# A hybrid encoder trunk on one core: the state space branch changes layout through memory, the next layer's preparation is cut into small steps, and the tokens are loaded ahead of the weights

## The chip, the cores and the metric

One core of a Trainium2 chip. TensorE (PE) multiplies, VectorE (DVE) and ScalarE (ACT) work on tiles of 128 partitions, GpSimd (POOL) fills and copies a little, SyncE (SP) issues most DMA transfers. The metric is the device time of one execution in microseconds, the median of several runs; a trace of one profiled execution stands beside it.

## The reference

Two layers over 512 tokens of width 1024, all in float32. Each layer is a gated mixer of three branches and a feed-forward part. The branch that the change touches is A, a diagonal complex state space layer of 16 groups of 16 channels:

```python
for l in range(DEPTH):
    h = rms_norm(x, norm1_g[l])
    z = h @ w_in[l]
    (u_ssm, dq, dk, dv, iq, ik, iw, rq, rk, rv, rg, gates) = split_cols(z)
    ya = s5_mixer(u_ssm, ...)        # scan of complex states, then GELU and a gated linear unit
    yb = dsa_mixer(...)              # indexer picks 128 keys per query, attention over them
    yc = retention_mixer(...)        # chunked retention, group norm, gate
    g = jax.nn.sigmoid(gates)
    merged = g_a * (ya @ w_proj_a[l]) + g_b * (yb @ w_proj_b[l]) + g_c * (yc @ w_proj_c[l])
    x = x + merged @ w_out[l]
    h2 = rms_norm(x, norm2_g[l])
    x = x + jnp.square(jax.nn.relu(h2 @ w_ff1[l])) @ w_ff2[l]
return rms_norm(x, final_norm_g)
```

## The kernel before

**Matmuls.** Activations are held feature-major (128 features by 512 tokens). Each product in float32 is made of three in a faster format: every operand is split in a high part and a residue. `wload` (L225) brings a block of weights: a DMA issued by SP into `raw`, a copy by ACT into `wh`, a subtraction by DVE into `wl`. Each of the three has three buffers, so SP can issue a load only when the residue three blocks back is done, and ACT can convert only when TensorE has used the block three back. `fm_blocks` (L261) and `tm_group` (L733) run over such blocks, 24 matmuls each.

**Order.** The order on every engine and queue is fixed at build time by a planner. It plays the program through with durations of its own, and at each point takes the ready instruction of highest priority, which is program order unless `tc.high_priority(n)` moves it ahead by n. Weight loads are moved ahead by 3000 (`LOOK`). A manual dependency of the kind `order` (L98) adds no wait on the chip; it keeps the planner from putting one instruction ahead of another on the same engine.

**Start.** L165 to L173 load constants and the tokens, half of the width by SP and half by ACT, in eight blocks `xt` of 256 KB. They are transposed, scaled and split, and the first projection follows.

**State space branch.** `s5_u` (L645) takes the branch's input from PSUM, 2 blocks of 128 channels by 512 tokens, and scales it by DVE. The state matmuls want another layout: the channels of four consecutive tokens (taps) stacked on the partitions, and the chunks of four tokens on the columns. `shuffle` (L639) makes it in 16 copies of 32 partitions by 128 columns per block, 12 by ACT and 4 by POOL, with a stride of four on the tokens. `s5_states` (L654) runs the state matmuls, the scans and the GELU and ends with the inverse shuffle, again 16 copies per block. `s5_glu` (L711) is the gated unit behind it, and runs after the first attention block, two projections and a top-k search.

In layer 0 the state matmuls come behind that layer's own preparation `s5_prep` (L514): rotation angles with their sines and cosines, and expanded input and output matrices. In layer 1 the preparation has been done during layer 0's feed-forward, and the state matmuls follow the keys directly.

**Feed-forward.** The hidden width is cut into eight slices. `ff1` (L1168) makes half a slice by a scheme of seven products of half size (84 matmuls of 256 columns, four PSUM banks of the pool `mx`, all there are); `ff2` (L1208) multiplies a slice into the residual stream `xp`, in two parts of four output blocks each, with one DVE addition per block (L1214). In layer 0, `s5_prep` for layer 1 is a generator of six steps, and L1258 runs one of them after each slice from the second on. Nothing keeps the planner from taking a step's instructions early.

Of the kernel before, what the change touches and what calls it, by code (L numbers as in the profile page):

```python
# [10 lines left out]
F32 = dt.float32  # L11
# [82 lines left out]
def build(tc, x, positions, norm1_g, w_in, lam_re, lam_im, log_step, b_re, b_im, c_re, c_im, ssm_d,  # L94
          glu_w, glu_b, ret_g, w_pa, w_pb, w_pc, w_out, norm2_g, w_ff1, w_ff2, fin_g, consts, out):
    nc = tc.nc
    pending, last = {}, {}
    order = mybir.DependencyInfo(mybir.DependencyClass.NoSync, mybir.DependencyReason.DATA)  # L98

    class Ordered:  # L100
# [5 lines left out]
        def __getattr__(self, name):  # L106
            fn = getattr(self._e, name)

            def call(*a, **k):
                r = fn(*a, **k)  # L110
                o = k["out"] if "out" in k else a[0]
                tag = pending.pop(o.tensor.name, None)
                if tag is not None:
                    if tag in last:
                        tc.add_manual_dep(r.ins, last[tag], order, reason="pages in program order")
                    last[tag] = r.ins.name
                return r

            return call
# [3 lines left out]
    with es:  # L123
# [4 lines left out]
        def f(t):  # L128
            return t.bitcast(F32)
# [36 lines left out]
        with tc.high_priority():  # L166
# [347 lines left out]
        def s5_prep(l, o):  # L514
# [4 lines left out]
            for hb in range(2):  # L519
# [3 lines left out]
                def v3(z):  # L523
                    return z.rearrange("p (i c) -> p i c", c=NCH)
# [3 lines left out]
                ve.tensor_tensor(v3(t), ib, rl[:, isl, None].to_broadcast([P, 4, NCH]), ALU.mult)  # L528
                ve.tensor_tensor(kk, ang, t, ALU.add)
                ve.tensor_scalar(kk, kk, 1.0 / TWO_PI, MAGIC, op0=ALU.mult, op1=ALU.add)  # L530
                ve.tensor_scalar(kk, kk, MAGIC, None, op0=ALU.subtract)
                for c in PI_PARTS:
                    stt(ang, kk, -c, ang, ALU.mult, ALU.add)
                ve.tensor_tensor(ang, ang, t, ALU.add)
# [21 lines left out]
            ve.tensor_tensor(bb[0], u1, u2, ALU.subtract)  # L556
            ve.tensor_tensor(u1v, bt[1], frb, ALU.mult)
# [16 lines left out]
            def expand(ar, ai, wr, wi, ops, re_t, im_t):  # L574

                for hb in range(2):
                    isl = slice(4 * hb, 4 * hb + 4)
                    sh = [P, 4, TAPS, 16]
                    for z, x1, x2, op in ((re_t[hb], ar, ai, ops[0]), (im_t[hb], ai, ar, ops[1])):
# [4 lines left out]
                        ve.tensor_tensor(w2, x2[:, isl, None, :].to_broadcast(sh), wi[:, isl, :, None].to_broadcast(sh), ALU.mult)  # L584
                        for a in range(2):
                            q = slice(64 * a, 64 * a + 64)
                            ov = z.rearrange("p (i j c) -> p i j c", j=TAPS, c=32)[q, :, :, 16 * a:16 * a + 16]
                            ve.tensor_tensor(ov, w1[q], w2[q], op)

            yield  # L590
            o.car, o.cai = [page(name="car") for _ in range(2)], [page(name="cai") for _ in range(2)]
            expand( ctv[0], ctv[1], prv[:, :, 1:], piv[:, :, 1:], (ALU.add, ALU.subtract), o.car, o.cai)
            vr, vi = [spage(name="vr") for _ in range(2)], [spage(name="vi") for _ in range(2)]
            expand( bbv[0], bbv[1], qrv, qiv, (ALU.subtract, ALU.add), vr, vi)
# [3 lines left out]
            for src, dst in ((vr, o.w1r), (vi, o.w1i)):  # L598
                for hb in range(2):
# [5 lines left out]
                    dst.append(z)  # L605
            yield
# [32 lines left out]
        def shuffle(n, o, i):  # L639
            if n % 4:  # L640
                copy(o, i)
            else:
                gp.tensor_copy(o, i)

        def s5_u(ps_b, b, rb, u):  # L645

            z = spage(name="s5u")
            ve.tensor_tensor(z, ps_b, rb, ALU.mult)
            for i in range(4):
                for j in range(TAPS):  # L650
                    shuffle(4 * i + j, u[32 * j:32 * j + 32, i * P:(i + 1) * P],
                            z[32 * i:32 * i + 32].rearrange("p (c j) -> p c j", j=TAPS)[:, :, j])

        def s5_states(l, o, u):  # L654
            gf = []
            for hb in range(2):
# [47 lines left out]
                for i in range(4):  # L704
                    for j in range(TAPS):
                        shuffle(4 * i + j, g[32 * i:32 * i + 32].rearrange("p (c j) -> p c j", j=TAPS)[:, :, j],
                                s[32 * j:32 * j + 32, i * P:(i + 1) * P])
# [3 lines left out]
        def s5_glu(l, gf, res):  # L711
# [8 lines left out]
            for m in range(2):  # L720
# [7 lines left out]
                copy(h, th, 0.25)  # L728
                stt(lo, th, 0.25, f(h), ALU.mult, ALU.subtract)
# [331 lines left out]
        def layer(l, nrm, o5):  # L1061
# [146 lines left out]
            def ff2(e, part):  # L1208
                hs, ls = sq[e]
                w2 = w_ff2[l][e * 512:(e + 1) * 512]  # L1210
                if e < NE - 1 or l + 1 < DEPTH:
                    for m, ps in fm_blocks(w2, 4 * part * P, 4, hs, ls, mm_ps):
                        m += 4 * part
                        ve.tensor_tensor(xp[m], xp[m], ps, ALU.add)  # L1214
# [38 lines left out]
            for e in range(NE):  # L1253
# [4 lines left out]
                if e:  # L1258
                    next(steps, None)
# [39 lines left out]
```

## Time and profile before

| | us |
|---|---|
| median of three runs | 1496.88 (1495.79 to 1500.19) |
| profiled execution, its own time | 1497.72 |
| its span | 1495.9 |
| TensorE matmuls busy | 1450.0 of the span |
| DVE busy | 1219.5 |
| ACT busy | 697.5 |
| POOL busy | 68.8 |

Times are counted from the start of the span. In a line of the windows the five busy times stand in the order matmuls, weight loads (which overlap them), DVE, ACT, POOL, with the number of instructions in brackets. An engine's idle time in front of an instruction is put down to what released it. A tile is known by the name in the program: `wh` and `wl` are the parts of a weight block, `mm` a product in PSUM, `f` the products of `ff1`, `u` and `s5f` the shuffled input and output of the state space branch, `ang`, `kk`, `pz`, `pw`, `s5m` and `w` tiles of the preparation, `xt` the tokens. A busy TensorE is not TensorE at its peak, so a stretch is also compared with one that does the same matmuls.

### The profile page before, as it was taken

To read this page: it belongs to the slowest core of one execution; us is meant where nothing else is said; L and a number is where in the kernel's file an instruction comes from. 1 tells how busy PE (TensorE), PEld (TensorE's weight loads), DVE (VectorE), ACT (ScalarE), POOL (GpSimd) and SP (SyncE) were. 2 spreads that over 40 slices of the span, in tenths; PEclk is the share of its full clock that TensorE was granted. 3 is DMA by queue.
4 is the path that set the end of the run, shared out by engine and by line. 5 is a ranking of instruction groups with operands and counts; after the bars stand their busy time and mean duration, and the time that the engine had idled before them with its cause. 6 is when DMAs were issued, how large, how long until landed. Compare 5 with 4: busy or idle time off the path is not lost.

```text
span 1495.9 us, 22071 instructions
## 1 busy us (share of the span) xinstructions
PE 1450.0 (97%) x8194; PEld 1279.6 (86%) x8194; DVE 1219.5 (82%) x2612; ACT 697.5 (47%) x1162; POOL 68.8 (5%) x131
## 2 busy tenths in 40 slices
PE   7999999999999999999999999999999999999997
PEld 6888898777887999889888889988788889998897
DVE  6887899985899878987775769998579788778877
ACT  5654643353534343344355753444445444344443
POOL 0311100000010000200001100000000000000000
PEclk9999999999999999999999999999999999999999
DMA  6331222223322333233442223223143323333333
GB/s 216 102 88 40 78 71 71 85 71 116 110 64 86 113 106 100 71 113 99 120 134 73 80 64 99 85 71 85 57 155 92 99 92 99 113 99 101 97 127 114
DMA packets 138992, 144.17 MB, mean 96 GB/s; under 512 B 11834, under 2 KB 131460, under 8 KB 138884
## 3 DMA queue, kind: packets, MB, share of 16 engines
q1 hardware_dynamic: 137556, 140.59, 31.1%
q10 hardware_dynamic: 1328, 2.17, 0.4%
q8 instruction: 64, 1.05, 0.3%
q14 instruction: 44, 0.36, 0.1%
HBM read 136.44 MB, written 6.29 MB: 95 GB/s over the span
## 4 chain that ended last, share of the span: by engine, by line
PE 84%; DVE 8%; ACT 3%; DMA 2%; issue 2%; POOL 0%; SPq 0%; POOLq 0%; DVEq 0%; ACTq 0%
PE mm L110 59%; PE f L110 16%; DVE wl L110 2%; ACT u L110 1%; DMA raw<-in_w_in_dram 1%; PE pv L110 1%; PE mx L110 1%; PE sp L110 1%; DMA raw<-in_w_ff_dram 1%; PE ry L110 1%; PE s5y L110 1%; PE pt L110 1%; ACT wh L110 1%; PE tr L110 1%; DVE raw L110 1%
## 5 line engine op out<-in xcount | busy, mean ns | idle before, releaser
L110 ACT ACTIVATE wh<-raw 128x1024 fp32r<-128x1024 f32 (+4 forms) x318 | 310.4, 978 | 513.3 <-PE mm L110 288.6
L110 DVE TENSOR_TENSOR wl<-raw,wh 128x1024 fp32r<-128x1024 f32 (+4 forms) x318 | 355.0, 1117 | 110.9 <-ACT wh L110 109.4
L110 PE MATMUL f<-xc,wh 128*128 128x256 f32 x1344 | 241.7, 280 | 0.2 <-ACT wh L110 0.2
L110 PE MATMUL mm<-sql,wh 128*128 128x512 f32 (+1 forms) x544 | 205.5, 378 | 1.8 <-DVE sql L110 1.8
L110 PE MATMUL mm<-sqh,wh 128*128 128x512 f32 (+1 forms) x544 | 205.3, 379 | 1.4 <-DVE fft L110 1.1
L110 PEld LDWEIGHTS f<-xc,wh 128*128 128x128 f32 x1344 | 204.7, 188 | 0.4 <-ACT wh L110 0.4
L110 PE MATMUL mm<-sqh,wl 128*128 128x512 f32 (+1 forms) x544 | 204.8, 380 | 0.0
L110 PE MATMUL f<-xc,wl 128*128 128x256 f32 x644 | 173.9, 280 | 0.2 <-DVE wl L110 0.2
L110 PE MATMUL mm<-xgh,wh 128*128 128x512 f32 x384 | 152.3, 397 | 0.0
L110 PE MATMUL mm<-xgl,wh 128*128 128x512 f32 x384 | 151.7, 395 | 0.0
L110 PE MATMUL mm<-xgh,wl 128*128 128x512 f32 x384 | 151.0, 394 | 0.0
L110 DVE TENSOR_TENSOR raw<-raw 128x256 f32<-128x256 f32 (+1 forms) x336 | 106.7, 328 | 28.9 <-DMA raw<-in_w_ff_dram 27.0
L110 PEld LDWEIGHTS mm<-sql,wh 128*128 128x128 f32 x544 | 102.1, 188 | 21.4 <-DVE sql L110 2.4
L110 PEld LDWEIGHTS mm<-sqh,wh 128*128 128x128 f32 x544 | 102.0, 188 | 20.3 <-issue 1.5
L110 PEld LDWEIGHTS f<-xc,wl 128*128 128x128 f32 x644 | 118.2, 188 | 1.2 <-DVE wl L110 0.8
L110 PEld LDWEIGHTS mm<-sqh,wl 128*128 128x128 f32 x544 | 102.2, 188 | 19.5
L110 PE MATMUL mm<-wh,xgh 128*128 128x384 f32 (+1 forms) x320 | 103.2, 336 | 3.4 <-ACT wh L110 2.7
L110 PE MATMUL mm<-wl,xgh 128*128 128x384 f32 (+1 forms) x320 | 105.2, 331 | 0.0
L110 PE MATMUL mm<-wh,xgl 128*128 128x384 f32 (+1 forms) x320 | 102.6, 333 | 1.0 <-DVE xgl L110 1.0
L110 DVE TENSOR_TENSOR x<-x,mm 128x512 f32<-128x512 f32 (+1 forms) x136 | 88.2, 648 | 9.3 <-PE mm L110 8.8
L110 PEld LDWEIGHTS mm<-xgh,wl 128*128 128x128 f32 x384 | 72.4, 188 | 15.4
L110 PEld LDWEIGHTS mm<-xgh,wh 128*128 128x128 f32 x384 | 72.4, 189 | 14.8
(385 smaller groups left out, 2670.5 us busy)
## 6 DMA issues: line engine op xcount, KB each, us to landing
raw<-in_w_ff_dram SPq DMA_DIRECT2D x76, 512.0 KB, 3.4
raw<-in_w_ff_dram SPq DMA_DIRECT2D x112, 256.0 KB, 2.8
raw<-in_w_in_dram SPq DMA_DIRECT2D x52, 512.0 KB, 3.7
raw<-in_w_in_dram SPq DMA_DIRECT2D x32, 384.0 KB, 3.3
raw<-in_w_out_dram SPq DMA_DIRECT2D x16, 512.0 KB, 3.4
xd<-x SPq DMA_DIRECT2D x16, 256.0 KB, 2.2
x<-xd SPq DMA_DIRECT2D x16, 256.0 KB, 4.9
raw<-in_w_proj_c_dram SPq DMA_DIRECT2D x8, 384.0 KB, 3.0
```

The source lines that it names most:

```text
L110: r = fn(*a, **k)
```

## The change

The change has three parts.

*Layout.* `shuffle` goes. `exchange` stores a 128 by 512 block to a tile in device memory and reads it back in four loads of 32 partitions, in runs of 128 numbers, all five issued by SP. The strided access moves to operations that were there: the product in `s5_u` writes its columns tap by tap, and the last operations of `s5_glu` read theirs tap by tap. In between the branch stays in the order of taps.

*Steps.* `s5_prep` is cut by further `yield`s into 35 steps, 33 of which hold work, and one is run after the residual addition of every output block from the second slice on (eight per slice). While a step is traced, `hold` names that addition, and every DVE instruction of the step is ordered behind it. Instructions of other engines are not held.

*Tokens.* The token loads are moved ahead by 100000 instead of the default.

```diff
-    pending, last = {}, {}
+    pending, last, hold = {}, {}, [None]
...
                 r = fn(*a, **k)
+                if hold[0] is not None and self._e is nc.vector:
+                    tc.add_manual_dep(r.ins, hold[0], order, reason="held back")
...
-        with tc.high_priority():
+        with tc.high_priority(100000):
             sc.dma_start(out=ct[:, :P], in_=consts[:, :P])
...
                 ve.tensor_tensor(v3(t), ib, rl[:, isl, None].to_broadcast([P, 4, NCH]), ALU.mult)
+                yield
                 ve.tensor_tensor(kk, ang, t, ALU.add)
                 ve.tensor_scalar(kk, kk, 1.0 / TWO_PI, MAGIC, op0=ALU.mult, op1=ALU.add)
                 ve.tensor_scalar(kk, kk, MAGIC, None, op0=ALU.subtract)
-                for c in PI_PARTS:
+                yield
+                for q, c in enumerate(PI_PARTS):
                     stt(ang, kk, -c, ang, ALU.mult, ALU.add)
+                    if q % 2:
+                        yield
...
             ve.tensor_tensor(bb[0], u1, u2, ALU.subtract)
+            yield
...
                         ve.tensor_tensor(w2, x2[:, isl, None, :].to_broadcast(sh), wi[:, isl, :, None].to_broadcast(sh), ALU.mult)
+                        yield
                         for a in range(2):
                             q = slice(64 * a, 64 * a + 64)
                             ov = z.rearrange("p (i j c) -> p i j c", j=TAPS, c=32)[q, :, :, 16 * a:16 * a + 16]
                             ve.tensor_tensor(ov, w1[q], w2[q], op)
+                        yield
...
-            expand( ctv[0], ctv[1], prv[:, :, 1:], piv[:, :, 1:], (ALU.add, ALU.subtract), o.car, o.cai)
+            yield from expand( ctv[0], ctv[1], prv[:, :, 1:], piv[:, :, 1:], (ALU.add, ALU.subtract), o.car, o.cai)
...
                     copy(z, ps)
                     dst.append(z)
+                    yield
...
-        def shuffle(n, o, i):
-            if n % 4:
-                copy(o, i)
-            else:
-                gp.tensor_copy(o, i)
+        bounce = [tc.dram_tile([P, SEQ], F32, name="bn%d" % q) for q in range(4)]
+
+        def exchange(q, o, z):
+
+            sy.dma_start(out=bounce[q], in_=z)
+            for j in range(TAPS):
+                sy.dma_start(out=o[32 * j:32 * j + 32].rearrange("p (i c) -> p i c", c=NCH),
+                             in_=bounce[q].rearrange("(i p) (j c) -> j p i c", p=32, c=NCH)[j])
+
+        def by_tap(z):
+
+            return z.rearrange("p (c j) -> p j c", j=TAPS)
...
             z = spage(name="s5u")
-            ve.tensor_tensor(z, ps_b, rb, ALU.mult)
-            for i in range(4):
-                for j in range(TAPS):
-                    shuffle(4 * i + j, u[32 * j:32 * j + 32, i * P:(i + 1) * P],
-                            z[32 * i:32 * i + 32].rearrange("p (c j) -> p c j", j=TAPS)[:, :, j])
+            ve.tensor_tensor(z.rearrange("p (j c) -> p j c", j=TAPS), by_tap(ps_b), by_tap(rb), ALU.mult)
+            exchange(b, u, z)
...
                 g = spage(name="s5f")
-                for i in range(4):
-                    for j in range(TAPS):
-                        shuffle(4 * i + j, g[32 * i:32 * i + 32].rearrange("p (c j) -> p c j", j=TAPS)[:, :, j],
-                                s[32 * j:32 * j + 32, i * P:(i + 1) * P])
+                exchange(2 + hb, g, s)
...
-                copy(h, th, 0.25)
-                stt(lo, th, 0.25, f(h), ALU.mult, ALU.subtract)
+                tv = th.rearrange("p (j c) -> p c j", j=TAPS)
+                copy(h.rearrange("p (c j) -> p c j", j=TAPS), tv, 0.25)
+                stt(lo.rearrange("p (c j) -> p c j", j=TAPS), tv, 0.25, f(h).rearrange("p (c j) -> p c j", j=TAPS), ALU.mult, ALU.subtract)
...
-                        ve.tensor_tensor(xp[m], xp[m], ps, ALU.add)
+                        r = ve.tensor_tensor(xp[m], xp[m], ps, ALU.add)
+                        if e:
+                            hold[0] = r.ins.name
+                            next(steps, None)
+                            hold[0] = None
...
-                if e:
-                    next(steps, None)
```

## Rows read from the trace of the kernel before

**Rows 1.** Page part 4, first line: the chain that ended last, by engine.
```profile
PE 84%; DVE 8%; ACT 3%; DMA 2%; issue 2%; POOL 0%; SPq 0%; POOLq 0%; DVEq 0%; ACTq 0%
```

**Rows 2.** Windows: stretch, length, busy time by engine, TensorE clock, DMA share, GB/s.
```profile
0.00:12.90 12.90, 3.94 (x17) 3.23 (x17) 2.48 (x6) 5.49 (x11) 1.81 (x11) 1.00 0.84 274
49.50:52.70 3.20, 1.68 (x10) 1.36 (x8) 0.79 (x4) 3.11 (x9) 0.00 (x0) 1.00 1.01 209
135.00:142.00 7.00, 4.33 (x24) 3.62 (x23) 6.22 (x13) 6.09 (x15) 1.75 (x5) 0.96 0.00 0
200.00:300.00 100.00, 97.79 (x494) 83.59 (x494) 98.06 (x254) 39.26 (x77) 4.04 (x4) 1.00 0.28 83
450.00:460.00 10.00, 6.95 (x28) 4.66 (x26) 10.00 (x23) 4.18 (x7) 0.00 (x0) 1.00 0.22 67
800.00:805.00 5.00, 2.72 (x17) 2.40 (x15) 0.58 (x1) 4.87 (x12) 0.00 (x0) 1.00 0.37 105
1210.55:1231.43 20.88, 20.88 (x135) 18.90 (x134) 16.82 (x30) 8.62 (x12) 0.00 (x0) 1.00 0.32 97
```

**Rows 3.** Timeline of the start: start us, us, engine, operation, [idle before <-releaser].
```profile
0.74 1.49 SPq L110 DMA_DIRECT2D raw<-in_w_in_dram  x3
...
6.01 0.47 SPq L110 DMA_DIRECT2D xt<-in_x_dram  x1
...
7.56 3.35 ACTq L110 DMA_DIRECT2D xt<-in_x_dram  x4
...
12.93 0.41 PE L110 MATMUL mm<-wh,xgh 128*128 128x292 f32 x1 [0.77 <-ACT xgh L110]
```

**Rows 4.** Tiles u and s5f: count, ns min/median/max, first and last start.
```profile
L110 ACT ACTIVATE u<-s5u x48: 420/427/444, 40.9 to 803.8; 32x128 f32<-32x128 f32 x48
...
L110 ACT ACTIVATE s5f<-s5g x48: 422/428/441, 135.8 to 855.8; 32x128 f32<-32x128 f32 x48
```

**Rows 5.** Timeline of DVE in layer 0: two waits for ACT.
```profile
52.64 0.29 DVE L110 TENSOR_TENSOR iks<-z,iks 128x128 fp32r<-128x128 f32 x1 [2.42 <-ACT iks L110]
...
172.47 0.55 DVE L110 TENSOR_TENSOR qs<-qT,qs 64x384 fp32r<-64x384 f32 x1 [3.26 <-ACT qs L110]
```

**Rows 6.** Chain in order of time: start us, length us, engine and tile.
```profile
354.45 55.16 PE mm L110 x239
...
700.10 1.75 PE w L110 x16
...
722.74 9.89 PE f L110 x84
...
743.63 3.49 PE kk L110 x32
...
1084.03 71.00 PE mm L110 x308
...
1440.33 9.90 PE f L110 x84
```

**Rows 7.** Groups on DVE, 410 to 760 us: first and last of the preparation.
```profile
L110 DVE SCALAR_TENSOR_TENSOR ang<-kk,ang 128x512 f32<-128x512 f32 x8 | 5.3, 672 | 0.0
...
L110 DVE TENSOR_TENSOR pz<-ct,vec 32x256 f32<-32x256 f32 x1 | 0.4, 422 | 0.0
```

**Rows 8.** Page part 6, DMA issues: count, KB each, median us to landing.
```profile
raw<-in_w_in_dram SPq DMA_DIRECT2D x32, 384.0 KB, 3.3
...
xd<-x SPq DMA_DIRECT2D x16, 256.0 KB, 2.2
...
pz<-in_ssm_b_re_dram SPq DMA_DIRECT2D x2, 64.0 KB, 4.1
```

**Rows 9.** Waits: engine and tile, waited for, us in total, times, longest.
```profile
SPq L110 <- DVE wl L110: 1025.0, 253, 20.2
...
ACT wh L110 <- DMA raw<-in_w_in_dram: 3.0, 3, 2.0
```

**Rows 10.** Timeline of ACT in layer 1: the first input copies.
```profile
792.82 5.30 ACT L110 ACTIVATE u<-s5u 32x128 f32<-32x128 f32 x12 [2.86 <-DVE s5u L110]
```

More of the change, by code (lines that the diff above doesn't have):

```diff
@@ L588, in expand @@
                             ve.tensor_tensor(ov, w1[q], w2[q], op)
+                        yield
             yield
             o.car, o.cai = [page(name="car") for _ in range(2)], [page(name="cai") for _ in range(2)]
-            expand( ctv[0], ctv[1], prv[:, :, 1:], piv[:, :, 1:], (ALU.add, ALU.subtract), o.car, o.cai)
+            yield from expand( ctv[0], ctv[1], prv[:, :, 1:], piv[:, :, 1:], (ALU.add, ALU.subtract), o.car, o.cai)
             vr, vi = [spage(name="vr") for _ in range(2)], [spage(name="vi") for _ in range(2)]
-            expand( bbv[0], bbv[1], qrv, qiv, (ALU.subtract, ALU.add), vr, vi)
+            yield from expand( bbv[0], bbv[1], qrv, qiv, (ALU.subtract, ALU.add), vr, vi)
             yield
```

## The prediction

> **What bounds the kernel now.** I read the page's chain first: TensorE's own work is most of the chain that ended last [rows 1]. So the time is TensorE's matmuls plus the places where it stands still, and only those places can give anything back. I then cut the span into stretches and looked for a PE busy time below the length of the stretch. In the feed-forward part of layer 1, a pitch (one block of 84 matmuls of 256 columns and one of 48 of 512) takes 20.88 us with PE busy for all of it [rows 2]. That is the rate to aim for. Losses stand where the change works: before the first matmul, 12.9 us with 3.94 busy; 3.20 us with 1.68 while ACT moves the state space input of layer 0; 7.00 with 4.33 while it moves the state space output; 5.00 with 2.72 at the same place in layer 1; 10.00 with 6.95 at the start of layer 0's feed-forward, where DVE is busy for all 10.00 [rows 2]. Between 200 and 300 us DVE is busy for 98.06 of 100, with the top-k search and the weight residues: there DVE sets the pace, so in the stretch ahead of it the time that counts is DVE's idle time, not PE's [rows 2].
>
> **Tokens first.** Now SP issues three weight loads, then three token blocks, and the fourth token block only at 6.01; ACT issues the other half at 7.56, behind its weight conversions; the first projection matmul comes at 12.93 [rows 3]. Afterwards all eight token blocks are issued by about 3 us, at 0.4 to 0.5 each on two queues, and the weights follow. The stretch moves 274 GB/s [rows 2]. Ahead of the first weight tile stand 2.10 MB of tokens, 0.07 MB of constants and the tile's own 0.30 MB: 2.47 MB at 274 GB/s is 9.0 us, from about 1.8 us on, so it lands at 10.8; with 0.7 for its conversion (an estimate) the first matmul stands at 11.5: 1.4 us gained. The token side alone (first transposes wait for a block issued 5.3 us late) would give up to 4. I take -2 between -4 and +1 (the tile lands late). The Trainium skill, "DMA: Bandwidth & Descriptors", section "Issuing engines are not separate DMA queues", says that loads issued by SP and ACT run on the same engines and interleave; this is the sum above. Were ACT's half on a path of its own, only 1.4 MB would stand ahead of the tile, and the gain would be near the 4. No row here separates the two.
>
> **State space input, layer 0.** Removed: per layer 24 ACT copies of 427 ns (10.3 us) and 8 on POOL, which is idle [rows 4]. The ACT copies hold back the key copies; DVE waits 2.42 us for them, and PE loses 1.5 us in that stretch [rows 2, 5]. The consumer of the moved data is far away (the first state matmul comes after all of layer 0's preparation), so the path through memory is covered by that work; without this cover it would cost its whole latency, worked out below. I take -2.1, between -2.4 and +2.
>
> **State space output, layer 0.** The same 24 ACT copies, at 428 ns [rows 4]. The first twelve stand in front of a weight conversion (PE loses 2.7 us in that stretch), the second in front of the query copies: DVE waits 3.26 us [rows 2, 5]. DVE sets the pace afterwards, so I count DVE's idle time, 3.3, and of PE's 2.7 at the first place 2.1, since other copies of ACT stand there too: -5.4, between 0 and -8 (a further stall of TensorE behind the late query copies goes as well). The consumer, the gated unit, stands behind two projections and a top-k search in program order: covered.
>
> **What an exchange costs.** One store of 256 KB and four loads of 64 KB, all on SP. The store's row is the one of x to memory: 2.2 us to landing; the loads write runs of 512 bytes, and their bound above is the 64 KB load in runs of 64 bytes, 4.1 us, below the store's 2.2 [rows 8]. I take 3. With issues of 0.4 each [rows 3] the data are there 0.4 + 2.2 + 1.6 + 3 = 7.2 us after the product, and SP is held for 4.2 us, as the loads wait for the store. Queued behind on SP stand the weight loads. They are issued when a raw buffer comes free, three conversions ahead; so two blocks lie between issue and conversion, 24 matmuls each: 2 x 5.5 us at 512 columns (a pitch less its 84 short matmuls, for 48 [rows 2, 6]), 2 x 4.1 at 384, less 3.3 for the landing [rows 8]: 7.7 and 4.9 us of slack. SP spends 1025 us waiting for such buffers, and ACT waited only 3.0 us for projection weights [rows 9]. One exchange is therefore hidden; two in a row, 8.4 us, exceed the smaller slack by 3.5. DVE and ACT now read strided operands in the input products and in the gated unit. No row prices that at 512 columns; between nothing and a doubling of eight DVE operations as wide as the angle steps, 672 ns [rows 7], it is 0 to 5 us on DVE. I take 0, as these stand beside matmuls.
>
> **State space input, layer 1.** Here the consumer is near. The first product ends at 792.82, where the copies start, and the last copy starts at 803.8 [rows 4, 10]. After the change SP does two exchanges in a row, so the second block is there at 792.8 + 4.2 + 7.2 = 804.2: no earlier. But ACT is free for the key and weight copies, and TensorE has the query projection to do. It loses 2.3 us now [rows 2]. I take -1.5, between -2.6 and +4 (matmuls ordered behind the data, or weights late by those 3.5). The output copies of layer 1 stand beside a TensorE that is busy throughout: nothing.
>
> **Preparation in steps.** Both layers run the same code from the last branch projection to the end of the 14th block of 84 matmuls. In layer 1, without preparation, from 1084.03 to 1450.23: 366.2 us. In layer 0 from 354.45 to 732.63: 378.2 [rows 6]. Of the 12.0 us more, 1.75 are sixteen transposes, true work [rows 6], and 0.4 are four more of that size: 9.8 us is what crowding costs. The angle work of both halves runs at the start of the feed-forward, where DVE is full. After the change each DVE operation of a step is ordered behind the residual addition of an output block, from the second of the eight hidden slices on. Queued behind it on DVE are the weight residues, for which TensorE waits. All the preparation is 33.1 us of DVE in 21 rows (first and last shown), 15.4 of it the angles [rows 7]. A pitch has room for 20.88 - 16.82 = 4.1 us [rows 2]. 33 steps with work in them, four to a pitch, ask for 4.0 on average: it fits, just. The ten angle steps ask for 15.4 in 2.5 pitches, 2.1 us too much in each, 5.2 in all; the weight residues lie ahead in priority and in buffers, and the angle work itself is not urgent. I take -7, between -9.8 and 0. The last step (small matmuls, 3.49 us on the chain, after the last block of 84 now [rows 6]) moves in among those blocks, which need all four of its PSUM banks: +1, between 0 and +4. The preparation's four 64 KB loads move with it; they take SP some 0.5 each to issue, as the tokens do, and land in 4.1 [rows 3, 8]: within the slack above. Its fills and copies on POOL meet an idle engine.
>
> **The sum.** -2 - 2.1 - 5.4 - 1.5 - 7 + 1 = -17.0 us against the profiled execution's 1497.72 (span 1495.9), which lies 0.8 us above the median of 1496.88. That is 1480.7; I say 1481. Ends of all terms together: -26.8 and +11.
>
> **The rivals.** First, *SP is held* (slower). A store can stand at the head of SP's queue before its product is ready, because the order on SP is fixed at build time. If it stands there 6 us, each of eight exchanges holds SP for 10.2 us, 3.9 beyond the mean slack of 6.3: +31 us, 1512. It decides from 2.1 us beyond the slack for each, where it eats the 17. For it speaks that SP is a queue of waits already; against it that weights arrive long before use [rows 9]. Second, *DVE has no room* (small gain): angles and residues collide, so the preparation gives half (-3.5), the last step costs 2, and half of the copies' 9.0 returns as waits for DVE between 200 and 300 us: -2 - 4.5 - 3.5 + 2 is -8: 1490. For it speaks the 4.0 against 4.1; against it that the angle work is now done where DVE has no room at all. Third, *all stalls go*: every term at its good end but the start's, -24.8: 1473. Fourth, *the change does not do what it says*, the angle work staying where it is: then the preparation gives nothing, -11.0 with nothing paid for the last step, 1487, beside the second and counted with it.
>
> **How the numbers follow.** Forecast 0.58; SP held 0.12; DVE has no room 0.18; all stalls go 0.12. Around each lies the reordering of every queue, which I cannot price, some 5 us. The range 1466 to 1497 leaves out most of the first rival and little below. A difference under 0.3%, 4.5 us, can't be told from no change. Faster: 0.58 + 0.12 + two thirds of 0.18, 0.82. Same: the rest of the second and a little of SP's, 0.08. Slower: 0.10.
>
> **What would show it.** Right: the first projection matmul near 11.5; no PE loss near 50 and 140; from the last branch projection of layer 0 to its 14th block under 372 us; angle work spread behind output blocks; weights never late after an exchange. Wrong: ACT or TensorE waiting for weight loads behind a store, state matmuls waiting for their input, a DVE full through the feed-forward with TensorE waiting for residues, or a hole at the last step.

## The result, and the profile after

The changed kernel takes 1487.64 us (median of 4 runs, 1487.29 to 1488.78) against 1496.34 us for the kernel before beside it: a ratio of 0.9926, with an interval of 0.991 to 0.9942. The profiled execution of after took 1487.64 us with a span of 1485.9, 10.0 us below the span of before. The forecast was 1481 us, 16 us less than before: the direction holds and the time lies in the range, but only half to two thirds of the gain came (8.7 us between the two medians, 11 by the ratio).

First the chain that ended last, by engine (page part 4, first line, of after). VectorE's part went from 8% to 4% [rows 1]; TensorE's own work is now nearly all of it.

```profile
PE 91%; DVE 4%; ACT 2%; DMA 2%; issue 1%; POOLq 0%; ACTq 0%; SPq 0%; DVEq 0%
```

Then stretches of after: length, then busy time and instructions of PE, PEld, DVE, ACT and POOL, the granted TensorE clock, DMA share, GB/s.

```profile
40.00:60.00 20.00, 20.00 (x118) 19.55 (x117) 20.00 (x80) 10.85 (x23) 2.69 (x2) 1.00 0.61 160
126.00:136.00 10.00, 9.69 (x63) 8.99 (x62) 3.22 (x6) 3.17 (x6) 0.00 (x0) 1.00 0.07 27
200.00:300.00 100.00, 100.00 (x497) 85.08 (x497) 97.60 (x241) 42.86 (x83) 4.92 (x3) 1.00 0.30 86
432.43:442.43 10.00, 10.00 (x86) 9.99 (x85) 9.59 (x15) 5.89 (x8) 0.00 (x0) 1.00 0.34 105
560.40:582.04 21.64, 21.15 (x135) 18.96 (x134) 19.54 (x39) 8.51 (x13) 0.53 (x1) 1.00 0.33 98
673.32:680.00 6.68, 6.68 (x46) 6.68 (x46) 2.35 (x8) 3.22 (x12) 0.00 (x0) 0.75 0.24 78
800.00:805.00 5.00, 5.00 (x31) 5.00 (x30) 4.61 (x7) 1.06 (x1) 1.04 (x2) 1.00 0.16 32
1242.48:1263.36 20.88, 20.88 (x133) 18.90 (x132) 17.11 (x31) 8.51 (x12) 0.00 (x0) 1.00 0.35 108
```

The holes named in [rows 2] are gone: nothing is lost between 40 and 60, nothing at 800, and the feed-forward of layer 0 begins with a full TensorE (432.43 to 442.43). New are three things. At 126 VectorE does 3.22 us of work in 10. A pitch in the middle of layer 0's feed-forward takes 21.64 us, where layer 1 still takes 20.88. And behind the last step the granted clock is 0.75 over 6.68 us.

The same in milestones. This is the chain of after in order of time (start, length, what), to be laid beside [rows 6]; the last two lines are from TensorE's timeline, the first matmul of the last branch projection in either layer.

```profile
669.96 3.54 PE kk L110 x32
...
716.86 9.89 PE f L110 x84
...
1430.64 9.90 PE f L110 x84
```
```profile
347.88 0.50 PE L110 MATMUL mm<-ybh,wh 128*128 128x512 f32 x1 [1.22 <-ACT ybh L110]
...
1074.14 0.50 PE L110 MATMUL mm<-ybh,wh 128*128 128x512 f32 x1 [1.22 <-ACT ybh L110]
```

Up to the last branch projection of layer 0 the kernel gained 6.6 us (354.45 to 347.88 [rows 6]); from there to the one of layer 1 it gained 3.3 (729.6 to 726.3); behind it nothing. This middle length, **from branch projection to branch projection**, holds all of the preparation, wherever its steps lie, and the mixer of layer 1; it is the measure for most experiments below.

### The profile page after: what moved, and what is told of

It is laid out like the page before. It is cut to its first block, busy times and chain, and to the rows that moved or that the text cites. A ratio compares the mean times of both kernels' runs of the same rounds, so it can differ in the third digit from the quotient of the medians.

```text
span 1485.9 us, 22022 instructions
## 1 busy us (share of the span) xinstructions
PE 1453.9 (98%) x8194; PEld 1282.3 (86%) x8194; DVE 1220.4 (82%) x2612; ACT 660.8 (44%) x1068; POOL 51.6 (3%) x99
## 4 chain that ended last, share of the span: by engine, by line
PE 91%; DVE 4%; ACT 2%; DMA 2%; issue 1%; POOLq 0%; ACTq 0%; SPq 0%; DVEq 0%
PE mm L110 64%; PE f L110 17%; PE mx L110 1%; PE pv L110 1%; PE sp L110 1%; DVE wl L110 1%; PE ry L110 1%; PE tr L110 1%; DMA xt<-in_x_dram 1%; PE pt L110 1%; PE s5y L110 1%; ACT wh L110 1%; PE rs L110 0%; PE kk L110 0%; DVE s5t L110 0%
## 5 line engine op out<-in xcount | busy, mean ns | idle before, releaser
L110 PEld LDWEIGHTS mm<-xgl,wh 128*128 128x128 f32 x384 | 72.4, 188 | 14.7
```

## Experiments

Each kernel stands beside runs of the kernel before on the same chip, and ratios are to those. A ratio of 0.001 is 1.5 us. Single profiles need care: a second profile of after, unchanged, reached its branch projection 3.8 us earlier and took 3.0 us more from there to the next. The first of these differences is TensorE's granted clock, as the stretch up to the branch projection shows in the two profiles, the first profile above:

```profile
0.00:347.88 347.88, 332.00 (x1728) 290.08 (x1728) 296.50 (x806) 164.37 (x317) 30.34 (x55) 0.98 0.33 96
```
```profile
0.00:344.12 344.12, 327.37 (x1728) 285.50 (x1728) 296.37 (x806) 164.33 (x317) 28.82 (x55) 0.99 0.33 97
```

The same 1728 matmuls kept TensorE busy 4.6 us longer at 0.98 than at 0.99; its idle time, length less busy, is 15.9 and 16.8 us. So idle time is compared below beside length. What rests on one stretch is shown in several kernels, or left as a hint.

The clock moves whole executions too. Over the 68 executions of the kernel before that stand beside the experiments, a mean clock lower by 0.001 goes with about 1.0 us more (an estimate, from a straight line through their recorded times and clocks). The mean clock of the executions of before lies between 0.990 and 0.992 on each chip, that of the other kernels between 0.992 and 0.996, so some us of a ratio can go with the clock. Whether a kernel raises its clock itself, or met it by chance, was not tested.

**The three parts alone.** The first kernel is before with one edit:

```diff
-        with tc.high_priority():
+        with tc.high_priority(100000):
```

> The kernel before with one edit alone: the token loads ahead of the weights. Theory 1 (the start gains what the trace of after shows by 30 us, 1.5 us, and nothing later gives it back): 1494.8 us. Rival (the first matmul comes earlier, but VectorE or ScalarE sets the pace of the first 60 us, so the gain is spent before the state space input ends): 1496.3, no change.

Measured: 0.9974 (0.9961 to 0.9987), 3.9 us less: more than Theory 1's 1.5, and the rival is out. The second is before with `exchange`, `by_tap` and the reordering in `s5_glu`, and nothing else of the diff (shortened; `[...]` stands for the indices):

```diff
-                    shuffle(4 * i + j, u[...], z[...])
+            exchange(b, u, z)
...
-                    shuffle(4 * i + j, g[...], s[...])
+                exchange(2 + hb, g, s)
```

> The kernel before with the state space input and output passed through memory, and nothing else. Theory 1 (the copies' stalls of layer 0 go as the trace of after shows: 2.3 us near 50, 2.9 near 140; layer 1 gives at most 1): 1490.5 us. Rival A (SP is held: in after it stands at a store of the state space output 24.3 us in three places, and this takes back what the copies gave): 1494 to 1497. Rival B (the layout is worth the whole change, the steps nothing): 1488.

Measured: 0.9964 (0.9951 to 0.9977), 5.4 us less, close to Theory 1's 5.8; both rivals lie outside. The third is before with the added `yield`s, `hold` and the loop of `ff2`, and nothing else (the `yield`s and `hold` are as in the diff of the change):

```diff
+                        if e:
+                            hold[0] = r.ins.name
+                            next(steps, None)
+                            hold[0] = None
...
-                if e:
-                    next(steps, None)
```

> The kernel before with the preparation of layer 1 in small ordered steps, and nothing else. Theory 1 (the steps remove the pile of angle work at the start of the feed-forward, but each held operation of VectorE stands ahead of a weight sum that ScalarE and TensorE wait for, so of 9.8 us only 2 to 3 come back): 1493.5 us. Rival A (the steps give the forecast 7 less 1, and it is the layout that gave little): 1490. Rival B (VectorE has no room at all, the steps cost as much as they free): 1496 or more.

Measured: 0.9981 (0.9967 to 0.9994), 2.8 us less, Theory 1's number; both rivals are out. The three add up to 12.1 us, within the interval of the whole (8.7 to 13.5). So no disturbance between the parts can be seen, though each part is known only to some 2 us. The tokens gave the forecast 2 us or more (1.9 to 5.8), the layout 5.4 of 9.0 and the steps 2.8 of 6.

**Which half of the layout.** From the layout kernel, the input goes back to copies (indices shortened):

```diff
-            ve.tensor_tensor(z.rearrange("p (j c) -> p j c", j=TAPS), by_tap(ps_b), by_tap(rb), ALU.mult)
-            exchange(b, u, z)
+            ve.tensor_tensor(z, ps_b, rb, ALU.mult)
+            for i in range(4):
+                for j in range(TAPS):
+                    shuffle(4 * i + j, u[...], z[...])
```

> The kernel before with the state space output alone passed through memory; the input is copied as before. Theory 1 (the output gives half of the layout's 5.4: in the trace of after VectorE's wait for the query copies is gone, but a wait for the state matmuls behind projections of TensorE stands in its place): 2 to 3 us less than before, a ratio of 0.998. Rival (the output gives what was forecast, 5.4, and the input nothing): 0.9964, as the whole layout.

Measured: 0.9993 (0.9978 to 1.0009): no difference. The rival's 0.9964 is out; Theory 1's 0.998 lies at the edge of the interval. The other half has the input through memory, and the output copied and `s5_glu` reading as before (indices shortened):

```diff
-                exchange(2 + hb, g, s)
+                for i in range(4):
+                    for j in range(TAPS):
+                        shuffle(4 * i + j, g[...], s[...])
```

> The kernel before with the state space input alone passed through memory; the output is copied as before. Theory 1 (the layout's gain, a ratio of 0.9964, is the input's, since the output alone gave 0.9993; in the first 60 us VectorE has no idle time left to give back later): 0.997, some 4 us less than before. Rival (each half alone only moves a wait, and the two pay together): 0.999 or more.

Measured: 0.992 (0.9897 to 0.9943), some 12 us by the ratio and 5.9 in the span of its profile, whose execution was its longest. The rival falls. Theory 1 has the direction; its size of 4 us is too small by the ratio. But about half of the 12 us goes with the clock: the mean clock of these executions is 0.9957, that of the kernel before beside them 0.9900, worth some 5.7 us by the estimate above. The layout kernel and its kernel before both have 0.9924. At equal clock the input alone gives some 6 us and both halves 5.4, so the gap between 0.992 and 0.9964 is no measure of what the output costs.

What holds is this: **the layout's gain is the input's; the output alone gives nothing that can be measured.** Two views show what the output's way through memory costs. First its price, by tiles (count, ns min/median/max, first and last start). In the kernel with the input alone:

```profile
L110 ACT ACTIVATE yah<-s5q x4: 612/630/679, 194.6 to 926.7; 128x512 fp32r<-128x512 f32 x4
L110 DVE SCALAR_TENSOR_TENSOR yal<-s5q,yah x4: 679/683/683, 196.3 to 927.7; 128x512 fp32r<-128x512 f32 x4
L110 DVE TENSOR_TENSOR s5u<-mx,rbc x4: 1071/1077/1131, 40.9 to 792.3; 128x512 f32<-128x512 f32 x4
```

and in the kernel with the output alone:

```profile
L110 ACT ACTIVATE yah<-s5q x4: 1104/1134/1222, 198.6 to 932.2; 128x512 fp32r<-128x512 f32 x4
L110 DVE SCALAR_TENSOR_TENSOR yal<-s5q,yah x4: 1048/1060/1086, 200.6 to 934.0; 128x512 fp32r<-128x512 f32 x4
...
L110 DVE TENSOR_TENSOR s5u<-mx,rbc x4: 672/684/691, 40.8 to 794.9; 128x512 f32<-128x512 f32 x4
```

The product in `s5_u` now reads operands that step over four elements of 4 bytes, 16 bytes; the two operations in `s5_glu` read, tap by tap, with a step of 128 elements, 512 bytes. Each costs VectorE 0.38 to 0.39 us more and ScalarE 0.50: 3.1 and 2.0 us over both layers. The Trainium skill, "SBUF — State Buffer", section "Door 1: The DMA port swizzle (why `[64,N]` ≈ `[32,N]`)", states that an access pays when it crosses to a new line of 16 bytes; with a step of 16 bytes or more every element does, and these rows agree. The product also reads from PSUM, and no run here separates the two memories.

Second, layer 1. The windows below are 16 us of its attention, from 33 to 17 us ahead of its last branch projection: the input alone, then the output alone.

```profile
1045.69:1061.69 16.00, 15.25 (x79) 12.88 (x78) 10.44 (x21) 9.19 (x19) 0.00 (x0) 1.00 0.17 53
```
```profile
1053.42:1069.42 16.00, 14.70 (x74) 11.85 (x72) 8.99 (x19) 8.42 (x18) 0.00 (x0) 1.00 0.23 70
```

With the output in memory TensorE does five matmuls fewer in this window, with 0.55 us less busy and at the same clock, with VectorE's work around it in another order (19 operations, not 21). The same cut gives 14.5 to 14.7 in the profiles of all eight other kernels with the output in memory, after among them, and 15.25 in before and in the two others that copy it. From the start of the 14th block of 84 matmuls in layer 0 to this branch projection before takes 361.4 us (722.58 to 1084.03), the input alone 358.7 (720.04 to 1078.69), the output alone 363.8 (722.64 to 1086.42), and two kernels with both and the same work in this stretch 363.1 (layout) and 362.0 (late last step, below). So in layer 1 the output costs some 2 us alone and 3.3 to 4.5 on top of the input; in the layout kernel a lower clock is part of it. That the build arrives at another order is shown; why it does was not tested.

**Is SP held?** This is after with the exchanges on POOL's queue:

```diff
-            sy.dma_start(out=bounce[q], in_=z)
+            gp.dma_start(out=bounce[q], in_=z)
```

and so for the four loads.

> The kernel after with the eight exchanges through memory issued from POOL's queue instead of SP's; nothing else. Theory 1 (SP's stands at these stores and loads, 24.3 us for three products and 13.2 us for data to land, cost nothing, as ACT waited only 4.4 us for projection weights): 1487.6 us, within 1.5. Rival (SP is held, the weights queued behind it come late and the output's half of the layout gave only 2 to 3 us instead of 5.4 for that reason): 1484 to 1485.

Measured: 0.9922 (0.9903 to 0.9942), as after. The waits of after say why: SP does stand at the head of a store for up to 9.6 us, as the first rival had it, but the weights behind it come in time.

```profile
SPq L110 <- DVE s5g L110: 24.3, 3, 9.6
...
ACT wh L110 <- DMA raw<-in_w_in_dram: 4.4, 2, 3.1
```

ScalarE waited 4.4 us for projection weights where it waited 3.0 before [rows 9]. The mechanism of that rival exists; its price does not.

**What the steps lack: the tie, the last step, or room?** First, after without the tie:

```diff
-                            hold[0] = r.ins.name
                             next(steps, None)
-                            hold[0] = None
```

> The kernel after without the tie of each step behind its output block's residual addition; the small steps, their place in the program, layout and tokens stay. Theory 1 (the tie puts the preparation's work between the sums of the next weights on VectorE, and a hole of some 2 us in each of five pitches comes from that order): faster than after, 1478 to 1483, and the holes at the blocks of 84 matmuls gone. Rival (the price is the work itself, and without the tie the angle work runs early where VectorE is full): 1490 or more, with TensorE waiting at the start of the feed-forward again.

Measured: 0.9938 (0.9921 to 0.9956); my theory named 1478 to 1483 us, and it is 1490. It falls. The first two pitches take 22.9 and 23.5 us again, as the rival said (20.9 in after): the tie does what it is for. Next, the last step back behind the last block (`count` starts at 0):

```diff
-                            next(steps, None)
+                            if count[0] < 34:
+                                next(steps, None)
+                            count[0] += 1
```

> The kernel after with one edit: the last step of the preparation (the sixteen small matmuls into one bank and what follows them) stays behind the last output block, as in the kernel before; the other 34 steps as in after. Theory 1 (in after the granted clock falls right behind these small matmuls, 0.75 over 6.68 us, and the pitch takes 1.6 us more; behind the last block of 84 matmuls it did not fall in the kernel before): 1486.0 us, 1.6 less than after, and no pitch behind them above 20.9. Rival (the clock falls wherever they stand, or the tail of the layer exposes what follows them): 1487.6 or more.

Measured: 0.9916 (0.9898 to 0.9935), no different from after. The two pitches behind the old place of these matmuls are back at 20.9 us in its profile, as Theory 1 said, but its 1.6 us is less than the interval can show. A second profile of after shows that the clock is not the whole price:

```profile
672.93:679.60 6.67, 5.70 (x48) 5.52 (x48) 2.36 (x8) 3.22 (x12) 0.00 (x0) 1.00 0.24 79
```

and, from the waits of the same stretch:

```profile
PE f L110 <- DVE s5m L110: 1.0, 1, 1.0
```

Here the clock stayed at 1.00 behind the same matmuls, yet TensorE stood still for 0.97 us until VectorE had emptied the last step's PSUM bank, and the pitch took 22.2 us instead of 22.5. In the first profile, at the lower clock, TensorE comes to that bank later and does not wait. So, by these two profiles, the slower clock mostly fills a wait. Both together are 1.3 to 1.6 us, and the kernel without them gains less than can be measured. Now fewer steps to a pitch, first five of each eight output blocks, then six:

```diff
-                        if e:
+                        if e and m in (0, 2, 4, 6, 7):
```

> The kernel after with the 35 steps spread over all 56 output blocks, five to each eight instead of eight, so that two and a half instead of four fall into a pitch; the last step falls behind the last block of 84 matmuls. Theory 1 (VectorE has no room: 16.8 us of its own work and 3.8 of steps fill a pitch of 20.9, and the pitches with steps take 21.7): with 2.4 us of steps the pitches come back to 20.9 to 21.1, 3 to 4 us less, and the clock's 1.6 as well: 1482.5 us. Rival (it is the order, a held operation ahead of a weight sum, and not the amount, so more pitches pay less each): 1486, only the clock's part.

Measured: 0.988 (0.986 to 0.99), 1483.2 us, beside 1487.5 for the kernel with the late last step on the same chip, at nearly the same mean clock (0.9940 and 0.9935). Theory 1 has the number; the rival's 1486 is out. Of thirteen pitches in its profile, its shortest execution, ten take 20.9 us, the others 21.3, 21.6 and 22.6.

```diff
-                        if e:
+                        if e and m in (0, 2, 3, 4, 6, 7):
```

> The kernel after with the steps on six of each eight output blocks instead of all, three to a pitch; the last step falls right behind the last block of 84 matmuls. Theory 1 (VectorE's room in a pitch decides, 4.1 us: four steps ask for 3.8 on average and more where they are angle work, three ask for 2.85): nearly all of what the spreading over five of eight gave, pitches of 20.9 to 21.2, 4 to 6 us less than after. Rival (any held step ahead of a weight sum costs some 0.2 us, however many stand in a pitch): half of it, pitches of 21.4, 2 to 3 us less than after.

Measured: 0.9897 (0.9878 to 0.9917), 1484.5 us, on one chip with after itself:

> The kernel after itself, unchanged, so that the other kernels of this call stand beside it on one chip. Every theory expects a ratio of 0.991 to 0.994 to the kernel before.

Measured: 0.9912 (0.9892 to 0.9933), 1487.0 us. So three to a pitch gives 2.4 us on the same chip. That is the rival's 2 to 3 us and not Theory 1's 4 to 6, and from the sixth on its pitches take 20.9 to 22.3 us, not 20.9 to 21.2. In the order of steps per pitch, four, three, two and a half, the middle length is 726.3 to 729.3 (after, twice) and 726.6 (late last step), 725.2, 721.7. Fewer tied steps in a pitch, less time: this is shown. That it is because VectorE has no room is not. Windows of the spread kernel, two pitches in the same place as 560.40 to 582.04 above:

```profile
533.10:554.01 20.91, 20.91 (x133) 18.93 (x132) 19.43 (x36) 9.77 (x15) 0.00 (x0) 1.00 0.32 101
554.01:575.29 21.28, 21.28 (x138) 19.11 (x136) 20.86 (x42) 9.62 (x15) 0.00 (x0) 1.00 0.31 99
```

VectorE is as busy in the first as in the 21.64 of after (19.43 and 19.54), and TensorE loses nothing. Two more pitches say it more strongly: one of after that holds 6.0 us of angle steps (its rows with `ang`, `angt` and `kk`), more than any other pitch of after, and one of the kernel with three to a pitch, which holds 2.3 us of steps (its rows with `pw`).

```profile
495.10:515.99 20.89, 20.89 (x134) 18.91 (x133) 20.17 (x37) 10.51 (x14) 0.00 (x0) 1.00 0.39 105
```
```profile
599.33:620.91 21.58, 21.19 (x133) 18.98 (x132) 18.96 (x38) 8.65 (x12) 0.00 (x0) 1.00 0.33 101
```

The fuller pitch loses nothing, the emptier one 0.7 us. So neither VectorE's share of a pitch nor the amount of steps against the 4.1 us of room tells a good pitch from a bad one. Where the work stands does; this is the timeline of after in the pitch from 560.40, VectorE, then ScalarE, then TensorE (start, length, operation, idle time before):

```profile
562.38 0.42 DVE L110 TENSOR_TENSOR raw<-raw 128x256 f32<-128x256 f32 x1
...
564.52 1.08 DVE L110 TENSOR_TENSOR wl<-raw,wh 128x896 fp32r<-128x896 f32 x1
565.52 0.84 DVE L110 TENSOR_TENSOR cai<-pw 64x256 f32<-64x256 f32 x2
566.40 0.62 DVE L110 TENSOR_TENSOR raw<-raw 128x128 f32<-128x128 f32 x2
568.08 3.38 DVE L110 TENSOR_TENSOR wl<-raw,wh 128x896 fp32r<-128x896 f32 x3 [1.07 <-ACT wh L110]
...
567.10 3.10 ACT L110 ACTIVATE wh<-raw 128x896 fp32r<-128x896 f32 x3 [5.83 <-issue]
...
568.11 1.06 PE L110 MATMUL f<-xc,wh 128*128 128x256 f32 x7 [0.49 <-ACT wh L110]
```

The three sums of one weight tile (`raw<-raw`) begin at 562.38 and end at 567.02. Between them stand two residues and a residual addition (left out above), a weight residue and a step (`cai`). VectorE has no gap in all that time; ScalarE has been idle for 5.83 us when it converts the tile at 567.10, and TensorE waits 0.49 of the pitch's extra 0.76 us for it. The trace names no releaser for ScalarE ("issue"), but the sums that it reads end 0.08 us earlier. Once the tile is converted, VectorE itself waits 1.07 us. In the bad pitch of three to a pitch the same order stands, with `car` for `cai`:

```profile
604.73 0.84 DVE L110 TENSOR_TENSOR car<-pw 64x256 f32<-64x256 f32 x2
605.60 0.62 DVE L110 TENSOR_TENSOR raw<-raw 128x128 f32<-128x128 f32 x2
...
606.31 1.90 ACT L110 ACTIVATE wh<-raw 128x896 fp32r<-128x896 f32 x2 [4.94 <-issue]
...
607.31 1.21 PE L110 MATMUL f<-xc,wh 128*128 128x256 f32 x8 [0.39 <-ACT wh L110]
```

In both a step of 0.84 us stands just ahead of the last sums of a weight tile, and TensorE waits 0.39 to 0.49 us for that tile. That is the "order" of the rival to the spreading. It is read from two traces; no kernel moved a step within a pitch to test it, so why fewer steps in a pitch cost less stays open: fewer may simply come to stand in such a place.

Last, the spread kernel without the tie:

> The spread kernel (steps on five of each eight output blocks) without the tie of each step behind its block's residual addition. Theory 1 (the tie's use is to keep the angle work out of the first two pitches, where without it TensorE lost 4.6 us in the trace): 2 to 4 us more than with the tie, 6 to 7 less than after at best. Rival (spread out in the program, the steps need no tie): within 1 us of the spread kernel, 7 to 8 us less than after.

Measured: 0.9938 (0.9918 to 0.9958), 1490.2 us, 3.2 more than after and 5.6 more than three to a pitch on the same chip. Its first two pitches take 23.9 and 23.5 us. The rival falls, and Theory 1 was still too mild: without the tie the spreading gains nothing (1490.1 us for four to a pitch without the tie, on another chip). The tie alone does gain: after took 1487.0 us, 3.2 less than this kernel on its chip. **The spreading pays only with the tie.**

The spread kernel is the fastest that ran: its interval (0.986 to 0.99) lies below that of after in the first result (0.991 to 0.9942) and just overlaps that of after beside three to a pitch (0.9892 to 0.9933); the ratios differ by some 5 to 7 us. Spreading with the input alone in memory was not run.

## Why the prediction came out as it did

The time lies in the range, and the terms can be set in two groups. Ahead of the branch projection of layer 0 the forecast took 9.5 us (tokens 2, input 2.1, output 5.4); the two profiles of after gained 6.6 and 10.3 there, and TensorE's idle time fell by 9.3 and 8.4. Behind it the forecast took 7.5 (1.5, 7, less 1); the profiles gained 3.3 and 0.3. So most of what is missing is missing behind the branch projection. The sum ahead of it came out by luck: one term gave more, another less. The forecast has no term for the granted clock, with which some 4 of the 13.2 us of after beside three to a pitch go (mean clock 0.9947 against 0.9906, by the estimate above).

*Tokens first*, -2 taken, 3.9 measured alone (1.9 to 5.8). The step "all eight token blocks are issued by about 3 us" is wrong, as the start of after shows against [rows 3]:

```profile
0.74 1.80 SPq L110 DMA_DIRECT2D xt<-in_x_dram  x4
1.66 1.28 ACT L110 ACT_TABLE_LOAD   x1 [1.66 <-PEq L1302]
2.58 2.65 SPq L110 DMA_DIRECT2D raw<-in_w_in_dram  x3
4.29 0.90 ACTq L110 DMA_DIRECT2D xt<-in_x_dram  x2
...
5.24 2.47 ACTq L110 DMA_DIRECT2D xt<-in_x_dram  x2
...
10.08 1.34 PE L110 MATMUL mm<-wh,xgh 128*128 128x292 f32 x4 [0.72 <-ACT wh L110]
```

ACT issues its tokens behind its own instructions, from 4.29 to 7.7, so the weight tile probably had less in front of it than I put there: the first projection matmul comes at 10.08, not 11.5. With the tokens alone TensorE's idle time ahead of the branch projection of layer 0 falls from 25.1 to 21.0 us. The size was off on the good side, for a reason I did not have.

*State space input, layer 0 and layer 1*, -2.1 and -1.5 taken: right in direction and about in size. These are the stretches up to the branch projection of layer 0 in before, with the input alone, and with the output alone:

```profile
0.00:354.45 354.45, 329.31 (x1728) 288.71 (x1729) 296.40 (x806) 181.09 (x363) 33.48 (x71) 0.98 0.30 88
```
```profile
0.00:351.65 351.65, 329.15 (x1729) 288.54 (x1729) 296.44 (x806) 173.68 (x341) 30.94 (x63) 0.99 0.31 92
```
```profile
0.00:354.17 354.17, 331.26 (x1728) 290.02 (x1728) 297.63 (x806) 171.83 (x339) 28.67 (x63) 0.98 0.31 91
```

With the input alone the branch projection comes 2.8 us earlier, and TensorE's idle time falls by 2.6, from 25.1 to 22.5. The middle length falls by 2.5. The hole at 800 is gone, and ScalarE waited for projection weights for 2.5 us, no more than before.

*State space output, layer 0*, -5.4 taken: this step failed. Alone the output moves the branch projection of layer 0 by 0.3 us. TensorE's idle time falls by 2.2 us, to 22.9, not by 5.4; and its 1728 matmuls are busy 1.95 us longer than in before, at a lower clock: the granted clock reads 0.50 from 183 to 189 us in that profile, and 0.51 over only 3.5 us, from 182.40, in before. VectorE's wait for the query copies did go [rows 5]. But I added VectorE's 3.3 us and TensorE's 2.1 as if what comes behind were free. In the trace of after VectorE waits in the same part for something else. These are its waits from 106 to 179.5 (us in total, times, longest):

```profile
DVE s5g L110 <- ACT s5g L110: 4.6, 2, 3.9
...
DVE gate L110 <- PE mm L110: 3.3, 2, 2.1
```

In before the first was 3.6 and the second 1.3 us. With the output alone, though, they are 3.6 and 1.9: there new waits take back only 0.6 us. So part of the loss is the clock, part is waits that differ from kernel to kernel, and the rest stays open. I had said that VectorE sets the pace from 200 on; ahead of that the two take turns: TensorE was busy for 9.69 of the 10 us from 126 in after, while VectorE had 3.22 us of work. For a stall that goes I asked what is late next, and answered without reading who has work left.

*State space output, layer 1*, nothing taken: it cost some 2 us, by the stretch from the 14th block to the branch projection (363.8 for 361.4). *Strided operands*, bounded by 0 and 5 us and taken at 0: 3.1 us on VectorE. The bounds were right; the choice is doubtful, for half of the operations stand in layer 0, and the first of them where VectorE is full (20.00 of the 20 us from 40). What they cost the kernel was not measured apart.

*What an exchange costs*, 7.2 us from product to data: right in size. The DMA issues of after for the output (KB each, median us to landing) are

```profile
bn<-s5g SPq DMA_DIRECT2D x4, 256.0 KB, 2.0
s5f<-bn SPq DMA_DIRECT2D x16, 64.0 KB, 2.0
```

and with four issues of 0.43 us between them the first block of layer 0 is there some 6 us after its store is issued.

*Preparation in steps*, -7 taken, and +1 for the last step: 2.8 measured alone (0.9 to 4.9). The pile at the start went as forecast; it was 5.7 us in two pitches (23.92 and 23.52 for 20.88), of the 9.8 counted as crowding; before has four later pitches of 22.2 to 22.6 as well, and after has its own. The step that failed is "33 steps with work in them, four to a pitch, ask for 4.0 on average: it fits, just". It weighs an amount against idle time, and that decides nothing in either direction. Of the angle steps, for which I feared 2.1 us too much in each pitch, 6.0 us cost nothing in one pitch (495.10 to 515.99) and 5.4 us cost 0.8 in the next, as much as 3.2 us of other steps did in three later pitches (21.6 to 21.8). What a step stands ahead of in VectorE's queue fits the traces better. The prediction's own sign failed too: from the last branch projection of layer 0 to the end of its 14th block it wanted under 372 us, and after takes 378.9 (347.88 to 726.75), or 375.3 without the small matmuls (3.54) that moved in, against 378.2 before. The last step was sized well: it does meet the banks it was said to meet (1.0 us), but moved away it changed nothing that can be measured.

*The rivals.* "DVE has no room" has the sum: the preparation gave half, and the copies' gain came back in part. Its 1490 is 2.4 us from the measured time, the forecast 6.6. But it put the returned waits between 200 and 300 us, where TensorE is busy for 100.00 of 100 in after, and it feared the angles, of which 6.0 us cost nothing in a full pitch. So its number is partly luck. "SP is held" was right that SP would stand at a store that is not ready, and wrong that anything waits for it. "The change does not do what it says" has the nearest number of all, 1487, and is out: the angle work moved. That is luck.

## What to carry to other kernels

Work that is tied to places in a full queue is not priced by its sum against the idle time: spread it thinly, keep the tie, and look at what each piece stands ahead of and who waits for that. When a stall is taken from one engine, find the engine that is a little later in the same stretch before counting the gain, and try the halves of a symmetric change one by one, since one may pay for the other. Before a few us are put down to an edit, compare the granted clock of the executions. A changed layout that makes a neighbour read or write with a stride has a price of its own at that neighbour.

## What the runs showed of the hardware

A 128x512 operation on fp32 took 1.08 us on VectorE instead of 0.68 when its operands step over four elements, 1.06 instead of 0.68 when one steps over 128, and 1.13 instead of 0.63 on ScalarE with that step of 128. A layout change by one store of 256 KB and four loads of 64 KB took some 6 us from the store's issue to the data, and went through SP's or POOL's queue at the same cost to the kernel (ratios 0.9926 and 0.9922).

The granted clock differs from execution to execution of one kernel. In after it had 0.98 and 0.99 up to the branch projection of layer 0, and the same 1728 matmuls were busy for 332.0 and 327.4 us. Behind the sixteen pairs of small matmuls (TensorE busy throughout, 3.5 us) it was 0.75 over 6.68 us in one execution of after, that is the lower of its two levels (1.2 GHz) for part of that stretch, and 1.00 in another; the pitch was as long within 0.3 us either way. Of the fourteen profiles six show 0.74 to 0.79 in such a stretch behind them and eight show 1.00.
